# Softmax denominators by two VectorE instructions a unit in place of a ones-matmul, and the last token tile's transposes earlier, in a one-core hybrid decoder block

## The chip, the cores and the metric

The kernel runs on one core of one Trainium2 chip. The metric is the device time of one execution in microseconds, taken as the median of the runs. Before the change it is 766.99 us over three runs (766.61 to 769.15).

## What is computed

A sequence of 1024 tokens, with 16 meta tokens in front (1040 in all), width 1024, goes through one block of two parallel mixers. Everything is float32. Cut to what matters here:

```
h = rmsnorm(x, norm_g);  proj = h @ w_in            # u_pool z_pool q k v z_attn f g_pool g_attn
y_pool = multiscale_pool(u_pool) * silu(z_pool)     # trailing means over 2, 4, 8, 16 tokens
log_f  = log_sigmoid(f + b_forget);  c = cumsum(log_f)
s = q.k / 8 + c[query] - c[key], causal;  p = softmax(s)   # 8 heads of 64
y_attn = (p @ v) * silu(z_attn)
merged = sigmoid(g_pool) * (y_pool @ w_up_pool) + sigmoid(g_attn) * (y_attn @ w_up_attn)
out = rmsnorm(x + merged @ w_out, final_norm_g)      # meta positions dropped
```

The change is about two pieces of it: the sum over the keys in the softmax, and the order of the work on the last tile of `h`.

## The kernel before

Every large product is made of three float32r matmuls: each operand is split into a high part and a low part, and high*high, high*low and low*high are accumulated in PSUM (`g_mm3`, L134 to L140; the matmul itself is L139). One call of `g_proj` is one piece: 24 matmuls over 8 slices of the width.

**The start (L352 to L445)** is written out by hand, for all engines: each engine runs its instructions in the order of the code. Nine token tiles `xt` (the last has 16 tokens) are loaded, scaled (`norm_scale`, VectorE, L176) and transposed on TensorE (`norm_t`, L187) into PSUM tiles: of the two halves of each tile, every third goes to `pn`, of which there is one buffer, the others to `pt`, of which there are two. ScalarE evicts the high part (`hh`, L189), VectorE the low part (`hl`, L190), and with that the buffer is free. Between the tiles stand twelve pieces: q, k and v of the first head pair over four quarters of the tokens, numbered n = 0 to 11 in the loop at L411. The tiles come in by the table of L420: the last tile, number 8, is transposed after n = 8 (v of tokens 512 to 768), and first needed by n = 9 (q of tokens 768 to 1040). After the loop the small weights `wf` of the forget gate are split on VectorE (`wfs`, L443 and L444), and `gates` (L447) multiplies by them (L456).

**Attention** has 16 units: head pair p, head e, half of the queries. Keys lie on partitions, queries on the free axis, in blocks of 128 keys: 5 blocks in a first half ("even" units), 9 in a second ("odd" units). For each block `qk` makes scores into `ps` (L540, L541, two buffers) and evicts them to `S` (ScalarE L549, VectorE L547 on the masked part), with a running maximum `m` on VectorE. `maxes` turns `m` into a maximum for each query (transpose L561, reduce L563, small steps, transpose L571 into a `pt` buffer). `soft` subtracts it (VectorE L580), takes exp (ScalarE L581), splits into `ph` (ScalarE L584) and `pl` (VectorE L585) and adds up `acc` on GpSimd (L590, L591, L593); `av` (L601) multiplies by V two blocks later. The blocks of `soft` of a unit are interleaved with those of `qk` of the next unit.

`finish` closes a unit: it evicts the output (L608, L609), folds the 128 rows of `acc` to 64 (ScalarE L614, VectorE L615), splits the fold into a high and a low half (ScalarE L616, VectorE L617), and leaves a function `total` that one or two steps into the next unit sums over the partitions with a matmul of ones (L621), copies the row out (ScalarE L623) and stores it to DRAM in `sums`.

TensorE's order is written by hand throughout (`manual_schedule`); between the attention steps `F.pull` hands it pieces of other projections (q, k, v of the next pair, then the pooled inputs and the gates, spilled to DRAM by L295 and L305), as many nanoseconds of them as a table of costs says, and `F.drain` (L687) runs what is left. The other engines are ordered by the framework's scheduler, which sees the data and the `after` hints (an order on one engine, no wait).

**The tail** reloads what was spilled, makes the pooling mixer, reads `sums` back as `lall`, takes reciprocals (L830), stores them in `recs`, multiplies them into the attention output (`attn_out`), and runs the two up projections (`up`, a = 0 for pool, 1 for attention) and the output projection (L892).

Of the kernel before, what the change touches and what calls it, by code (L numbers as in the profile page):

```python
# [19 lines left out]
H = 8  # L20
# [19 lines left out]
NRC = 2  # L40
REC0 = 2
EVAC = (((0, 1),), ((0,), (1,)))
# [3 lines left out]
def r32(ap):  # L46
    return ap.bitcast(F32)
# [7 lines left out]
def tile_hybrid_block(ctx, tc, x, meta, norm_g, w_in, b_forget, pool_w, pool_scale,  # L55
# [355 lines left out]
    for n, (kind, t0, t1) in enumerate(todo):  # L411
        if n + 4 < 9:
            xts[n + 4] = norm_load(n + 4)
        if kind == "q":
            run(q_piece(0, wq, max(NM, t0), t1))
        elif kind == "k":
            run(k_piece(0, wk, t0, t1))
        else:
            run(v_piece(0, wv, t0, t1))
        i = {0: 2, 1: 3, 3: 4, 4: 5, 6: 6, 7: 7, 8: 8}.get(n)  # L420
        if i is not None:
            norm_t(i, xts[i], ntok(i))
# [16 lines left out]
    nc.sync.dma_start(psc, pool_scale[0].rearrange("(g c) -> c g", c=128))  # L439
    wf = sm.tile([128, KO, H], F32, name="wf", bufs=1)  # L440
    nc.sync.dma_start(wf, w_in2[:, :, COL_F:COL_F + H])
    wfs = sm.tile([128, KO, 2 * H], F32R, name="wfs", bufs=1)
    nc.vector.tensor_copy(wfs[:, :, :H], wf)  # L443
    nc.vector.tensor_tensor(wfs[:, :, H:], wf, r32(wfs[:, :, :H]), op=ALU.subtract)  # L444
    SM.close()  # L445

    def gates():  # L447
# [13 lines left out]
        for b in range(NB):  # L461
            nc.tensor.transpose(pt[:, b * 16:(b + 1) * 16], fT[:, KS[b]:KS[b] + KB], ident[:16, :16])
        z, lf, u, d, one, car = [sm.tile([KB, NB, H], F32, name=n, bufs=1) for n in ("fz", "lf", "fu", "fd", "fo", "car")]
        pv = pt[:, :NB * 16].rearrange("p (b j h) -> p b j h", j=2, h=H)
# [33 lines left out]

    exps, dves = [], []
    sums = dr.tile([H, SEQ], F32, name="sums")  # L500
    recs = dr.tile([H, SEQ], F32, name="recs")
    for p in range(4):
        spill["y", p] = dr.tile([128, SEQ], F32, name=f"sp_y{p}")

    class Unit:
# [19 lines left out]
        def qk(self, b):  # L525
# [22 lines left out]
            if f0 < 512:  # L548
                nc.scalar.activation(s[:kb, f0:], ps[:kb, f0:], AF.Identity, bias=nb_)  # L549
            S0 = self.S[0]  # L550
# [23 lines left out]
        def soft(self, b):  # L574
            kb, c0 = self.kb[b], self.c0[b]
            s = self.S[b]
            if b == 0:
                self.po = psO.tile([128, 512], F32, name="po")
                self.acc = ap_.tile([KB, 512], F32, name="acc", bufs=2)
            nc.vector.tensor_tensor(s[:kb, c0:], s[:kb, c0:], self.pm[:kb, c0:], op=ALU.subtract)  # L580
            exps.append(nc.scalar.activation(s[:kb, c0:], s[:kb, c0:], AF.Exp))  # L581
# [3 lines left out]
            dves.append(nc.vector.tensor_tensor(pl[:kb, c0:], s[:kb, c0:], r32(ph[:kb, c0:]), op=ALU.subtract))  # L585
            self.P[b] = (ph, pl)
            acc, S0 = self.acc, self.S[0]
            if b == 1:
                if c0:
                    nc.gpsimd.tensor_copy(acc[:, :c0], S0[:, :c0])  # L590
                nc.gpsimd.tensor_tensor(acc[:, c0:], S0[:, c0:], s[:, c0:], op=ALU.add)  # L591
            elif b > 1:
                nc.gpsimd.tensor_tensor(acc[:kb, c0:], acc[:kb, c0:], s[:kb, c0:], op=ALU.add)  # L593
            if b >= LAG:
                self.av(b - LAG)
# [8 lines left out]
        def finish(self):  # L604
# [5 lines left out]
            nc.sync.dma_start(spill["y", self.p][hr, self.q0:self.q0 + 512], t[hr])  # L610
            fold = ap_.tile([128, 512], F32R, name="ph", bufs=NPH)
            up_ = r32(ap_.tile([128, 512], F32R, name="pl", bufs=NPH))
            nu = KB - 64
            nc.scalar.copy(up_[:nu], acc[64:])  # L614
            nc.vector.tensor_tensor(acc[:nu], acc[:nu], up_[:nu], op=ALU.add)  # L615
            nc.scalar.activation(fold[:64], acc[:64], AF.Copy)  # L616
            nc.vector.tensor_tensor(fold[64:], acc[:64], r32(fold)[:64], op=ALU.subtract)  # L617

            def total():
                pr = psT.tile([128, 512], F32, name="pt")  # L620
                nc.tensor.matmul(pr, onesr, fold, start=True, stop=True)  # L621
                ls = ap_.tile([1, 512], F32, name="ls")
                nc.scalar.copy(ls, pr[:1])  # L623
                h = 2 * self.p + self.e
                nc.sync.dma_start(sums[h:h + 1, self.q0:self.q0 + 512], ls)

            return [total]

    def merged(a, c, extra=()):
        extra = list(extra)  # L630
        out_ = []
        for lst in (a, c):
            tot = sum(s[0] for s in lst) or 1
            acc = 0.0
            for s in lst:
                out_.append(((acc + 0.5 * s[0]) / tot, s))
                acc += s[0]
        for i, (_, (w, dve, pe, f)) in enumerate(sorted(out_, key=lambda t: t[0])):
            f()
            if i >= REC0 and extra:  # L640
                extra.pop(0)()
            F.pull(max(0.0, PACE * dve - pe))
# [22 lines left out]
    units[0].maxes(FIRST)  # L665
    late = []
    for i, u in enumerate(units):
        nxt = units[i + 1] if i + 1 < 16 else None
        F.now = i
        if nxt is not None and nxt.p != u.p:  # L670
            F.until(f"q{nxt.p}", f"k{nxt.p}")
        merged(list(nxt.a_steps()) if nxt else [], list(u.c_steps()), late)
        for b in range(u.nb - LAG, u.nb):
# [5 lines left out]
        if nxt is not None:  # L679
            nxt.maxes()  # L680
        late = u.finish()
        if nxt is not None and nxt.p != u.p:
            F.until(f"v{nxt.p}")
            pair_fill(nxt.p + 1)
    for f in late:
        f()
    F.drain()  # L687
# [47 lines left out]
    def attn_out(p):  # L735
        rc = btile("rc")
        for e in range(2):
            h = 2 * p + e
            after(nc.sync.dma_start(rc[rows(e)[0]], recs[h:h + 1, :].to_broadcast([64, SEQ])), stores[-1])
        nc.vector.tensor_tensor(Y[p], Y[p], rc, op=ALU.mult)  # L740
# [217 lines left out]
```

## Time and profile before

| | |
|---|---|
| profiled execution, its own time | 769.11 us |
| its span, first to last instruction | 767.4 us |
| runs: median, lowest, highest | 766.99, 766.61, 769.15 us |
| TensorE matmul busy | 751.6 us, 98% |
| TensorE weight loads busy | 638.5 us, 83% |
| VectorE busy | 497.1 us, 65% |
| ScalarE busy | 394.6 us, 51% |
| GpSimd busy | 278.1 us, 36% |
| mean granted TensorE clock | 0.997 |

Engines in the rows are PE (matmuls), PEld (weight loads), DVE (VectorE), ACT (ScalarE), POOL (GpSimd) and SP (the DMA queue of the sync engine); L139 is a line of the kernel. A row of a timeline has the start and the length in microseconds, the engine, the line, the operation, the tiles written and read, and in brackets the idle time before it and what ended that. A row of a group has, after the bar, the busy time of the group, the mean nanoseconds of one instruction, and the idle time before them. The clock column of a table of stretches is the share of full speed that TensorE was granted.

### The profile page before, as it was taken

Reading aid. Unit: us, or ns where it says so; the run is one execution under the profiler, and the core shown is the slowest. Engines: PE = TensorE matmul, PEld = TensorE weight load, DVE = VectorE, ACT = ScalarE, POOL = GpSimd, SP = SyncE. Lnnn points to the kernel's source line nnn. Section 1 sums busy time; section 2 is a strip of 40 time slices with the busy share of each in tenths; the row PEclk is TensorE's granted clock in tenths of the full one; section 3 lists DMA queues with packets and bytes.
Section 4 is the critical chain, followed back from the end, with each engine's and each line's share of the span. In section 5 each row is a group of like instructions: output and inputs, shape, how many; then the busy total and the mean of one; then the engine's idle time right before and its main releaser. Section 6 shows DMA issues by size and latency. Waiting matters only on the chain.

```text
span 767.4 us, 10526 instructions
## 1 busy us (share of the span) xinstructions
PE 751.6 (98%) x3762; PEld 638.5 (83%) x3762; DVE 497.1 (65%) x933; ACT 394.6 (51%) x756; POOL 278.1 (36%) x227
## 2 busy tenths in 40 slices
PE   8999999999999999999999999999999999999996
PEld 6996989988888898888988888888888688888885
DVE  5653578659779888598688866882465566434232
ACT  6652556456566655665655556551744554323112
POOL 4321235346326435433354263342374122322111
PEclk9999999999999999999999999999999999999999
DMA  9301122231221222221223232339357654523331
GB/s 304 73 18 39 28 82 74 67 97 49 62 58 52 72 75 70 77 63 41 77 62 103 71 103 62 103 108 373 123 176 177 233 176 128 191 83 113 107 110 55
DMA packets 73782, 79.33 MB, mean 103 GB/s; under 512 B 5473, under 2 KB 56673, under 8 KB 73730
## 3 DMA queue, kind: packets, MB, share of 16 engines
q1 hardware_dynamic: 68976, 63.46, 27.0%
q10 hardware_dynamic: 4754, 15.21, 6.0%
q8 instruction: 29, 0.48, 0.3%
q14 instruction: 23, 0.19, 0.1%
HBM read 57.58 MB, written 21.07 MB: 102 GB/s over the span
## 4 chain that ended last, share of the span: by engine, by line
PE 79%; DVE 8%; ACT 2%; issue 2%; DMA 2%; POOL 1%; POOLq 0%; DVEq 0%; SPq 0%; ACTq 0%
PE pj L139 57%; PE pj L892 12%; PE po L601 4%; PE ps L541 2%; PE ps L540 2%; DVE pl L585 1%; DVE S L580 1%; DMA rl<-sp_gp 1%; PE pj L456 1%; DVE ka L243 1%; POOL yl L722 1%; ACT S L549 1%; DMA rc<-recs 1%; DVE m L556 1%; DVE acc L615 0%
## 5 line engine op out<-in xcount | busy, mean ns | idle before, releaser
L139 PE MATMUL pj<-hh,whi 128*128 128x512 f32 (+4 forms) x768 | 179.9, 362 | 1.7 <-ACT hh L189 1.1
L139 PE MATMUL pj<-hl,whi 128*128 128x512 f32 (+4 forms) x768 | 178.0, 361 | 0.0
L139 PE MATMUL pj<-hh,wlo 128*128 128x512 f32 (+4 forms) x768 | 175.7, 360 | 0.0
L128 POOL TENSOR_TENSOR wlo<-raw,whi 128x1024 fp32r<-128x1024 f32 x37 | 91.7, 2478 | 223.7 <-ACT whi L127 90.5
L139 PEld LDWEIGHTS pj<-hh,whi 128*128 128x128 f32 x768 | 132.8, 190 | 19.6 <-ACT hh L189 1.2
L139 PEld LDWEIGHTS pj<-hh,wlo 128*128 128x128 f32 x768 | 133.2, 190 | 18.2
L139 PEld LDWEIGHTS pj<-hl,whi 128*128 128x128 f32 x768 | 132.5, 190 | 17.7
L585 DVE TENSOR_TENSOR pl<-S,ph 128x512 fp32r<-128x512 f32 (+4 forms) x112 | 87.1, 793 | 19.9 <-ACT ph L584 18.9
L593 POOL TENSOR_TENSOR acc<-acc,S 128x272 f32<-128x272 f32 (+4 forms) x80 | 77.5, 969 | 12.6 <-ACT S L581 6.6
L549 ACT ACTIVATE S<-ps,negc 128x400 f32<-128x400 f32 (+2 forms) x96 | 49.1, 515 | 46.7 <-DVE S L547 40.4
L581 ACT ACTIVATE S<-S 128x512 f32<-128x512 f32 (+4 forms) x112 | 49.4, 477 | 29.0 <-DVE S L580 28.9
L556 DVE TENSOR_TENSOR m<-m,S 128x272 f32<-128x272 f32 (+4 forms) x80 | 46.7, 583 | 22.3 <-ACT S L549 21.0
L584 ACT ACTIVATE ph<-S 128x512 fp32r<-128x512 f32 (+4 forms) x112 | 52.4, 478 | 11.6 <-PE po L601 10.8
L580 DVE TENSOR_TENSOR S<-S,pt 128x512 f32<-128x512 f32 (+4 forms) x112 | 51.7, 498 | 0.8
L892 PE MATMUL pj<-woh,gl 128*128 128x512 f32 (+1 forms) x136 | 51.8, 381 | 0.0
L892 PE MATMUL pj<-wol,gh 128*128 128x512 f32 (+1 forms) x136 | 51.6, 379 | 0.0
L892 PE MATMUL pj<-woh,gh 128*128 128x512 f32 (+1 forms) x136 | 51.6, 379 | 0.0
L816 POOL TENSOR_TENSOR gl<-rl,gh 128x512 fp32r<-128x512 f32 x16 | 23.2, 1454 | 72.3 <-ACT gh L815 72.3
L294 ACT ACTIVATE st<-pj 128x512 f32<-128x512 f32 x48 | 28.4, 592 | 39.7 <-PE pj L139 21.5
L127 ACT ACTIVATE whi<-raw 128x1024 fp32r<-128x1024 f32 x37 | 39.0, 1054 | 17.2 <-PE pj L139 10.6
L812 DVE TENSOR_TENSOR rl<-pj,rl 128x512 f32<-128x512 f32 x32 | 22.0, 689 | 31.8 <-PE pj L139 28.4
L540 PE MATMUL ps<-qa,ka 128*128 128x512 f32 (+4 forms) x112 | 36.4, 325 | 2.2 <-ACT S L549 2.1
(168 smaller groups left out, 1136.4 us busy)
## 6 DMA issues: line engine op xcount, KB each, us to landing
raw<-in_w_in_dram SPq DMA_DIRECT2D x40, 512.0 KB, 4.0
sp_gp<-st SPq DMA_DIRECT2D x16, 256.0 KB, 2.0
sp_ga<-st SPq DMA_DIRECT2D x16, 256.0 KB, 4.5
rl<-sp_gp ACTq DMA_DIRECT2D x8, 512.0 KB, 3.8
rl<-sp_ga ACTq DMA_DIRECT2D x8, 512.0 KB, 4.6
rawo<-in_w_out_dram SPq DMA_DIRECT2D x8, 512.0 KB, 3.1
xr<-in_x_dram SPq DMA_DIRECT2D x8, 512.0 KB, 4.3
xt<-in_x_dram SPq DMA_DIRECT2D x7, 512.0 KB, 8.3
```

The source lines that it names most:

```text
L127: nc.scalar.activation(hi, raw, AF.Copy)
L128: (eng or nc.gpsimd).tensor_tensor(lo, raw, r32(hi), op=ALU.subtract)
L139: nc.tensor.matmul(ps, a, b, start=(i == 0), stop=(i == len(seq) - 1))
L540: nc.tensor.matmul(ps[:kb, c0:], ka[:, k0:k0 + kb], qa[:, q0 + c0:q0 + 512], start=True, stop=False)
L549: nc.scalar.activation(s[:kb, f0:], ps[:kb, f0:], AF.Identity, bias=nb_)
L556: nc.vector.tensor_tensor(m[:kb, c0:], m[:kb, c0:], s[:kb, c0:], op=ALU.max)
L580: nc.vector.tensor_tensor(s[:kb, c0:], s[:kb, c0:], self.pm[:kb, c0:], op=ALU.subtract)
L581: exps.append(nc.scalar.activation(s[:kb, c0:], s[:kb, c0:], AF.Exp))
L584: nc.scalar.activation(ph[:kb, c0:], s[:kb, c0:], AF.Copy)
L585: dves.append(nc.vector.tensor_tensor(pl[:kb, c0:], s[:kb, c0:], r32(ph[:kb, c0:]), op=ALU.subtract))
L593: nc.gpsimd.tensor_tensor(acc[:kb, c0:], acc[:kb, c0:], s[:kb, c0:], op=ALU.add)
L892: nc.tensor.matmul(ps[:, :c1 - c0], mg[k][a][:, r], wo[k][b][:, c0:c1], start=(k == 0 and n == 0), stop=(k == KO - 1 and n == 2))
```

## The change

In words: `finish` no longer folds `acc` and no longer leaves a `total`. It transposes `acc` on VectorE in 32x32 blocks into an `mt` tile, reduces it to 128x16, and stores that in `sums`; an `after` puts the transpose behind the unit's last `pl` in VectorE's order. The tail reads `sums` back in four DMAs, one a head pair, sums over the four partition groups, takes the reciprocal, transposes back and stores `recs`. The first exp of a unit is put, in ScalarE's order, behind the last score eviction that was recorded before it. The last token tile is transposed after n = 7 in place of n = 8. `wf` is loaded after n = 4 and split after n = 8. The five small gate tiles become one, so that the tail can reuse its buffer.

The short description of the change also names "four pool up projections ahead of attention's". The diff does not touch `up` or its loop, and TensorE's order there is the same in both kernels: pool's projections 0, 1 and 2, then attention's 0, then alternating.

```
-        i = {0: 2, 1: 3, 3: 4, 4: 5, 6: 6, 7: 7, 8: 8}.get(n)
+        i = {0: 2, 1: 3, 3: 4, 4: 5, 6: 6, 7: 7}.get(n)
         if i is not None:
             norm_t(i, xts[i], ntok(i))
+        if n == 7:
+            norm_t(8, xts[8], ntok(8))
...
+        if n == 4:
+            wf = sm.tile([128, KO, H], F32, name="wf", bufs=1)
+            nc.sync.dma_start(wf, w_in2[:, :, COL_F:COL_F + H])
+        if n == 8:
+            wfs = sm.tile([128, KO, 2 * H], F32R, name="wfs", bufs=1)
+            nc.vector.tensor_copy(wfs[:, :, :H], wf)
+            nc.vector.tensor_tensor(wfs[:, :, H:], wf, r32(wfs[:, :, :H]), op=ALU.subtract)
...
-                nc.scalar.activation(s[:kb, f0:], ps[:kb, f0:], AF.Identity, bias=nb_)
+                sevs.append(nc.scalar.activation(s[:kb, f0:], ps[:kb, f0:], AF.Identity, bias=nb_))
...
             exps.append(nc.scalar.activation(s[:kb, c0:], s[:kb, c0:], AF.Exp))
+            if b == 0:
+                after(exps[-1], sevs[-1])
...
-            fold = ap_.tile([128, 512], F32R, name="ph", bufs=NPH)
-            up_ = r32(ap_.tile([128, 512], F32R, name="pl", bufs=NPH))
-            nu = KB - 64
-            nc.scalar.copy(up_[:nu], acc[64:])
-            nc.vector.tensor_tensor(acc[:nu], acc[:nu], up_[:nu], op=ALU.add)
-            nc.scalar.activation(fold[:64], acc[:64], AF.Copy)
-            nc.vector.tensor_tensor(fold[64:], acc[:64], r32(fold)[:64], op=ALU.subtract)
-
-            def total():
-                pr = psT.tile([128, 512], F32, name="pt")
-                nc.tensor.matmul(pr, onesr, fold, start=True, stop=True)
-                ls = ap_.tile([1, 512], F32, name="ls")
-                nc.scalar.copy(ls, pr[:1])
-                h = 2 * self.p + self.e
-                nc.sync.dma_start(sums[h:h + 1, self.q0:self.q0 + 512], ls)
-
-            return [total]
+            at = ap_.tile([KB, 512], F32, name="mt")
+            after(nc.vector.transpose(at, acc), dves[-1])
+            r = sm.tile([128, 16], F32, name="sr")
+            nc.vector.tensor_reduce(r, at.rearrange("p (j b) -> p j b", b=32), axis=AX.X, op=ALU.add)
+            nc.sync.dma_start(sums[4 * self.p + 2 * self.e + self.half], r)
...
-    lall = sm.tile([128, 64], F32, name="lall", bufs=1)
-    nc.sync.dma_start(lall, sums.rearrange("h (a b) -> (h a) b", b=64))
-    after(nc.vector.reciprocal(lall, lall), split2)
-    nc.sync.dma_start(recs.rearrange("h (a b) -> (h a) b", b=64), lall)
+    for p in range(4):
+        nc.sync.dma_start(lall[32 * p:32 * p + 32],
+                          sums[4 * p:4 * p + 4].rearrange("u (a r) j -> r u a j", r=32))
+    after(nc.vector.tensor_reduce(rall.rearrange("p (u j) -> p u j", u=4), lall.rearrange("p u a j -> p u j a"),
+                                  axis=AX.X, op=ALU.add), split2)
+    nc.vector.reciprocal(rall, rall)
+    nc.vector.transpose(fin[:, 320:], rall)
+    nc.sync.dma_start(recs.rearrange("(b p) r -> p b r", p=128), rect)
```

Three places show what this does to the engines' order. First TensorE in the start, before the change, from the transposes of tile 7 (`pn`, then `pt`, 128 columns) to the first matmuls of piece n = 9 (272 columns); the 256-column rows between are piece n = 8, and L256 are two transposes of V:

```order
L187 MATMUL pn<-ident,xt 128x128 x4
L187 MATMUL pt<-ident,xt 128x128 x4
L256 MATMUL pj<-ident,vt 128x128 x2
L139 MATMUL pj<-hh_112,whi 128x256 x4
L139 MATMUL pj<-hh_113,whi 128x256 x4
L139 MATMUL pj<-hl_114,whi 128x256 x4
L139 MATMUL pj<-hl_115,whi 128x256 x4
L139 MATMUL pj<-hh_112,wlo 128x256 x4
L139 MATMUL pj<-hh_113,wlo 128x256 x4
L187 MATMUL pt<-ident,xt 128x16 x4
L187 MATMUL pn<-ident,xt 128x16 x4
L139 MATMUL pj<-hh_112,whi 128x272 x4
```

And the same stretch of TensorE in the changed kernel, where the lines of the code have other numbers:

```order
L186 MATMUL pn<-ident,xt 128x128 x4
L186 MATMUL pt<-ident,xt 128x128 x4
L186 MATMUL pt<-ident,xt 128x16 x4
L186 MATMUL pn<-ident,xt 128x16 x4
L255 MATMUL pj<-ident,vt 128x128 x2
L138 MATMUL pj<-hh_112,whi 128x256 x4
L138 MATMUL pj<-hh_113,whi 128x256 x4
L138 MATMUL pj<-hl_114,whi 128x256 x4
L138 MATMUL pj<-hl_115,whi 128x256 x4
L138 MATMUL pj<-hh_112,wlo 128x256 x4
L138 MATMUL pj<-hh_113,wlo 128x256 x4
L138 MATMUL pj<-hh_112,whi 128x272 x4
```

The eight 16-column transposes of the last tile moved ahead of piece n = 8, directly behind those of tile 7, so that all of piece n = 8 stands behind them. On VectorE the low-part evictions of the last tile (`hl`, 128x4x16) moved with them, ahead of two V evictions; everything before them is as it was.

Second, VectorE at the end of the second unit (0, 0, second half), before, from the last maximum of the next unit to the transposed maximum `pt`:

```order
L556 TENSOR_TENSOR m<-m,S 128x16
L561 STREAM_TRANSPOSE mt<-m 128x512
L615 TENSOR_TENSOR acc<-acc,pl 64x512
L563 TENSOR_REDUCE mr<-mt 128x16
L565 COPY mx<-mr 64x16 x2
L617 TENSOR_TENSOR ph<-acc,ph 64x512
L566 TENSOR_TENSOR ms<-mr,mx 128x16
L568 COPY my<-ms 32x16 x4
L569 TENSOR_TENSOR mz<-ms,my 128x16
L571 STREAM_TRANSPOSE pt<-mz 128x512
```

And in the changed kernel:

```order
L561 TENSOR_TENSOR m<-m,S 128x16
L566 STREAM_TRANSPOSE mt<-m 128x512
L568 TENSOR_REDUCE mr<-mt 128x16
L570 COPY mx<-mr 64x16 x2
L619 STREAM_TRANSPOSE mt<-acc 128x512
L571 TENSOR_TENSOR ms<-mr,mx 128x16
L621 TENSOR_REDUCE sr<-mt 128x16
L573 COPY my<-ms 32x16 x4
L574 TENSOR_TENSOR mz<-ms,my 128x16
L576 STREAM_TRANSPOSE pt<-mz 128x512
```

Two instructions for the sums stand among those of the maximum in both; they are others, and a little later.

Third, ScalarE at the start of the third unit (0, 1, first half), before; `S<-S` is an exp, `S<-ps` the eviction of scores of the next unit (the first two stand behind these rows), `st` and `whi` belong to the filling projections:

```order
L614 COPY pl<-acc 64x512
L616 ACTIVATE ph<-acc 64x512
L304 ACTIVATE st<-pj 128x384
L608 ACTIVATE t<-po 64x512
L581 ACTIVATE S<-S 128x512
L581 ACTIVATE S<-S 128x400
L584 ACTIVATE ph<-S 128x512
L304 ACTIVATE st<-pj 128x272
L584 ACTIVATE ph<-S 128x400
L581 ACTIVATE S<-S 128x272
```

And in the changed kernel:

```order
L303 ACTIVATE st<-pj 128x384
L615 ACTIVATE t<-po 64x512
L126 ACTIVATE whi<-raw 128x1024
L586 ACTIVATE S<-S 128x400
L303 ACTIVATE st<-pj 128x272
L586 ACTIVATE S<-S 128x272
L586 ACTIVATE S<-S 128x144
L586 ACTIVATE S<-S 128x16
L554 ACTIVATE S<-ps,negc 128x512
L586 ACTIVATE S<-S 128x512
L591 ACTIVATE ph<-S 128x512
L591 ACTIVATE ph<-S 128x400
```

The two copies of the fold are gone, and the unit's first exp stands behind the first score eviction of the next unit, with the exps of the other four blocks ahead of it. It is so in the eight even units; in the odd units the eviction that the exp stands behind is one of its own scores, long done.

More of the change, by code (lines that the diff above doesn't have):

```diff
@@ L40 @@
 NRC = 2
-REC0 = 2
 EVAC = (((0, 1),), ((0,), (1,)))
@@ L439, in tile_hybrid_block @@
     nc.sync.dma_start(psc, pool_scale[0].rearrange("(g c) -> c g", c=128))
[L440 to L444, printed above, removed]
     SM.close()
@@ L462, in gates @@
             nc.tensor.transpose(pt[:, b * 16:(b + 1) * 16], fT[:, KS[b]:KS[b] + KB], ident[:16, :16])
-        z, lf, u, d, one, car = [sm.tile([KB, NB, H], F32, name=n, bufs=1) for n in ("fz", "lf", "fu", "fd", "fo", "car")]
+        fz = sm.tile([KB, 384], F32, name="fz", bufs=1)
+        z, lf, u, d, one = [fz[:, n * NB * H:(n + 1) * NB * H].rearrange("p (b h) -> p b h", h=H) for n in range(5)]
+        car = sm.tile([KB, NB, H], F32, name="car", bufs=1)
         pv = pt[:, :NB * 16].rearrange("p (b j h) -> p b j h", j=2, h=H)
@@ L497, in tile_hybrid_block @@
     pwl = sm.tile([128, 4, 128], F32R, name="pwl", bufs=1)
-    exps, dves = [], []
-    sums = dr.tile([H, SEQ], F32, name="sums")
-    recs = dr.tile([H, SEQ], F32, name="recs")
+    exps, dves, sevs = [], [], []
+    sums = dr.tile([16, 128, 16], F32, name="sums")
+    recs = dr.tile([256, 32], F32, name="recs")
     for p in range(4):
@@ L610, in finish, with merged @@
             nc.sync.dma_start(spill["y", self.p][hr, self.q0:self.q0 + 512], t[hr])
-            fold = ap_.tile([128, 512], F32R, name="ph", bufs=NPH)
-            up_ = r32(ap_.tile([128, 512], F32R, name="pl", bufs=NPH))
-            nu = KB - 64
[L614 to L617, printed above, removed]
-            def total():
-                pr = psT.tile([128, 512], F32, name="pt")
-                nc.tensor.matmul(pr, onesr, fold, start=True, stop=True)
-                ls = ap_.tile([1, 512], F32, name="ls")
-                nc.scalar.copy(ls, pr[:1])
-                h = 2 * self.p + self.e
-                nc.sync.dma_start(sums[h:h + 1, self.q0:self.q0 + 512], ls)
-            return [total]
-    def merged(a, c, extra=()):
-        extra = list(extra)
+            at = ap_.tile([KB, 512], F32, name="mt")
[3 more added lines that the diff above has]
+            nc.sync.dma_start(sums[4 * self.p + 2 * self.e + self.half], r)
+    def merged(a, c):
         out_ = []
@@ L637, in merged @@
                 acc += s[0]
-        for i, (_, (w, dve, pe, f)) in enumerate(sorted(out_, key=lambda t: t[0])):
+        for _, (w, dve, pe, f) in sorted(out_, key=lambda t: t[0]):
             f()
-            if i >= REC0 and extra:
-                extra.pop(0)()
             F.pull(max(0.0, PACE * dve - pe))
@@ L665, in tile_hybrid_block @@
     units[0].maxes(FIRST)
-    late = []
     for i, u in enumerate(units):
@@ L671, in tile_hybrid_block @@
             F.until(f"q{nxt.p}", f"k{nxt.p}")
-        merged(list(nxt.a_steps()) if nxt else [], list(u.c_steps()), late)
+        merged(list(nxt.a_steps()) if nxt else [], list(u.c_steps()))
         for b in range(u.nb - LAG, u.nb):
@@ L680, in tile_hybrid_block @@
             nxt.maxes()
-        late = u.finish()
+        u.finish()
         if nxt is not None and nxt.p != u.p:
@@ L684, in tile_hybrid_block @@
             pair_fill(nxt.p + 1)
-    for f in late:
-        f()
     F.drain()
@@ L737, in attn_out @@
         for e in range(2):
-            h = 2 * p + e
-            after(nc.sync.dma_start(rc[rows(e)[0]], recs[h:h + 1, :].to_broadcast([64, SEQ])), stores[-1])
+            rw = recs.rearrange("(h c) r -> h (c r)", h=H)[4 * e + p:4 * e + p + 1]
+            after(nc.sync.dma_start(rc[rows(e)[0]], rw.to_broadcast([64, SEQ])), stores[-1])
         nc.vector.tensor_tensor(Y[p], Y[p], rc, op=ALU.mult)
@@ L827, in tile_hybrid_block @@
     silu(zp[2])
-    lall = sm.tile([128, 64], F32, name="lall", bufs=1)
-    nc.sync.dma_start(lall, sums.rearrange("h (a b) -> (h a) b", b=64))
-    after(nc.vector.reciprocal(lall, lall), split2)
-    nc.sync.dma_start(recs.rearrange("h (a b) -> (h a) b", b=64), lall)
+    fin = sm.tile([128, 384], F32, name="fin", tag="fz", bufs=1)
+    lall = fin[:, :256].rearrange("p (u a j) -> p u a j", u=4, a=4)
+    rall = fin[:, 256:320]
+    rect = fin[:, 320:].rearrange("p (b r) -> p b r", b=2)
+    for p in range(4):
[6 more added lines that the diff above has]
+    nc.sync.dma_start(recs.rearrange("(b p) r -> p b r", p=128), rect)
     pool_chain(1)
```

## The prediction

> **What bounds the kernel now.** I read the page first: the busy times, the chain that ended last, then the groups by line.
>
> ```profile
> PE 751.6 (98%) x3762; PEld 638.5 (83%) x3762; DVE 497.1 (65%) x933; ACT 394.6 (51%) x756; POOL 278.1 (36%) x227
> PE 79%; DVE 8%; ACT 2%; issue 2%; DMA 2%; POOL 1%; POOLq 0%; DVEq 0%; SPq 0%; ACTq 0%
> ...
> L621 PE MATMUL pt<-ph,onesr 128*128 128x512 f32 x16 | 6.4, 401 | 0.0
> ```
>
> TensorE is busy for 98% of the span and makes 79% of the chain. A busy TensorE need not be at its peak, so I looked at its waits, and at a stretch of the chain with nothing but matmuls of 512 columns.
>
> ```profile
> PE ps L540 <- ACT S L549: 2.1, 3, 1.1
> ...
> PE pj L456 <- DVE wfs L444: 0.9, 1, 0.9
> ...
> 601.13 70.96 PE pj L139 x304
> ```
>
> Named waits of TensorE are a few single microseconds. 304 matmuls in 70.96 us are 233 ns each: what one more or one fewer 512-column matmul costs where TensorE never waits. In attention it hardly does. The first block of the third unit shows why:
>
> ```profile
> 151.04 1.17 DVE L580 TENSOR_TENSOR S<-S,pt 128x512 f32<-128x512 f32 x2
> ...
> 151.77 1.06 ACT L581 ACTIVATE S<-S 128x512 f32<-128x512 f32 x2 [1.37 <-DVE S L580]
> ...
> 153.38 1.61 DVE L585 TENSOR_TENSOR pl<-S,ph 128x512 fp32r<-128x512 f32 x2
> 154.01 0.40 PE L540 MATMUL ps<-qa,ka 128*128 128x512 f32 x1
> ...
> 155.68 0.68 ACT L549 ACTIVATE S<-ps,negc 128x512 f32<-128x512 f32 x1
> ...
> 158.65 0.69 DVE L554 TENSOR_TENSOR m<-S 128x512 f32<-128x512 f32 x1 [3.58 <-ACT S L549]
> ...
> 164.21 0.39 PE L601 MATMUL po<-ph,V 128*128 128x512 f32 x1
> ```
>
> The exps run from 151.77, the first `pl` is made by about 154.2 (half of the two from 153.38), and TensorE needs it behind the row at 164.21, 10 us later. So what is taken from TensorE is time saved; what is taken from ScalarE or VectorE in attention saves almost nothing, and costs nothing until such slack is used up.
>
> **The ones-matmuls.** Sixteen go. At 233 ns each that is 3.7 us, all of it on the path, since their group had no idle time before it (0.0). The last one cost more:
>
> ```profile
> 513.10 0.26 PE L601 MATMUL po<-pl,V 128*128 128x16 f32 x1
> 513.38 0.50 PE L621 MATMUL pt<-ph,onesr 128*128 128x512 f32 x1
> 513.72 1.32 PE L139 MATMUL pj<-hh,whi 128*128 128x512 f32 x5
> ```
>
> It started 0.28 us behind the matmul before it, which has 16 columns, and gave way after 0.34: 0.3 to 0.4 us beyond its 233 ns. Sum: **-4.1 us** (ends -3.5 and -4.5).
>
> **The fold and its successors.** Per unit:
>
> ```profile
> L615 DVE TENSOR_TENSOR acc<-acc,pl 64x512 f32<-64x512 f32 x16 | 12.4, 778 | 0.5 <-ACT pl L614 0.2
> L617 DVE TENSOR_TENSOR ph<-acc,ph 64x512 fp32r<-64x512 f32 x16 | 11.8, 738 | 0.3
> L561 DVE STREAM_TRANSPOSE mt<-m 128x512 f32<-128x512 f32 x16 | 11.3, 706 | 0.3
> L563 DVE TENSOR_REDUCE mr<-mt 128x16 f32<-128x512 f32 x16 | 10.8, 675 | 0.2
> L616 ACT ACTIVATE ph<-acc 64x512 fp32r<-64x512 f32 x16 | 10.1, 633 | 16.2 <-DVE acc L615 14.5 <-DVE ms L566 1.7
> L614 ACT COPY pl<-acc 64x512 f32<-64x512 f32 x16 | 9.9, 618 | 2.7 <-PE po L601 2.4
> L623 ACT COPY ls<-pt 1x512 f32<-1x512 f32 x16 | 9.0, 563 | 5.1 <-POOL pwl L678 5.0
> ```
>
> VectorE loses 778 + 738 and gains 706 + 675 ns, the prices of the same two operations on `m`: 0.14 us less, 16 times 2.2 us. ScalarE loses 633 + 618 + 563 ns, 29 us in all. Neither engine is late for TensorE, so I count 0 (ends -1.5, if the ScalarE wait of 2.1 us above shrinks, and +0.5). The new transpose sits in VectorE's queue in front of the next unit's `pt` and all its exps, and waits for GpSimd's `acc`. In the tightest unit, the sixth:
>
> ```profile
> 245.87 3.85 POOL L593 TENSOR_TENSOR acc<-acc,S 128x400 f32<-128x400 f32 x4
> ...
> 252.08 0.71 DVE L561 STREAM_TRANSPOSE mt<-m 128x512 f32<-128x512 f32 x1
> ```
>
> `acc` ends at 249.72 and the transpose comes after `mt` at 252.08, so this wait is 2.4 us from biting. The `sums` stores become 128 short pieces, and four reloads wait on SP for such stores to land, with weight loads and spills queued behind them. In no row of its waits does TensorE wait for a weight split of these pieces (`whi`, `wlo`) or for a spilled bank, so a few microseconds on SP stay hidden: 0. The tail's extra reduce and transpose fall into VectorE's wait for `u` behind the reciprocals:
>
> ```profile
> 548.91 1.24 DVE L757 TENSOR_TENSOR s<-u 128x1039 f32<-128x1039 f32 x1 [3.83 <-DMA u<-sp_u]
> ```
>
> **The first exp.** In the third unit it moves from 151.77 to behind the eviction of scores that TensorE finishes at about 154.7: some 4 us later, against 10 us of slack. The eviction itself comes earlier than its 155.68. The merged gate tiles change no wait. Count 0.
>
> **The last tile, sooner.** Here the change gives back. These are rows of the start, with the clock of the same stretch:
>
> ```profile
> 42.62 1.19 PE L139 MATMUL pj<-hh,whi 128*128 128x256 f32 x8
> ...
> 43.23 1.39 DVE L176 SCALAR_TENSOR_TENSOR xt<-xt,rstd,gb 16x512 f32<-16x512 f32 x2 [0.65 <-POOL rstd L111]
> ...
> 45.52 0.69 DVE L190 TENSOR_TENSOR hl<-pn,hh 128x512 fp32r<-128x512 f32 x1
> ...
> 46.27 0.42 PE L187 MATMUL pn<-ident,xt 16*128 16x16 f32 x4 [0.24 <-DVE hl L190]
> ...
> 47.77 1.27 PE L139 MATMUL pj<-hh,whi 128*128 128x272 f32 x8 [1.08 <-ACT hh L189]
> ...
> 52.26 1.31 PE L139 MATMUL pj<-hh,whi 128*128 128x272 f32 x8
> ...
> 55.54 1.25 PE L139 MATMUL pj<-hh,whi 128*128 128x272 f32 x8
> ...
> 59.66 1.54 PE L456 MATMUL pj<-hh,wfs 128*16 128x384 f32 x8 [0.86 <-DVE wfs L444]
> ```
>
> ```profile
> 49.00:50.00 1.00, 1.00 (x8) 1.00 (x7) 0.00 (x0) 0.00 (x0) 0.00 (x0) 0.58 0.00 0
> 50.00:51.00 1.00, 1.00 (x6) 1.00 (x6) 0.00 (x0) 0.27 (x1) 0.00 (x0) 0.50 0.00 0
> 51.00:52.00 1.00, 1.00 (x6) 1.00 (x6) 0.00 (x0) 0.79 (x1) 0.00 (x0) 0.50 0.08 16
> 52.00:53.00 1.00, 1.00 (x8) 1.00 (x7) 0.00 (x0) 0.49 (x2) 0.40 (x1) 0.71 0.00 0
> ```
>
> Before, piece n = 8 ran from 42.62 to about 45.6, and only then came the last tile's transposes. The second four of them need the one `pn` buffer, which VectorE frees with the row that ends at 46.21; they start at 46.27. Nothing ahead of that row on VectorE or ScalarE moved. In the new order TensorE stands ready at about 42.4, waits for the scaled tile until about 43.9 (the first half of the 43.23 row), and then for the same 46.27, with all of piece n = 8 behind. The piece then starts at about 46.8 and ends, after the same 3.0 us, at 49.8, where n = 9 can start at once: 2.0 us later than 47.77. The wait of 0.86 us for `wfs` goes, because its split now comes three pieces earlier than its use. Without the clock: **+1.1 us**.
>
> The clock: in these rows about 3.4 us stand at half speed, behind a stretch in which TensorE had 1.08 us idle and transposes. It cost 4.49 us for n = 9 (47.77 to 52.26) against 3.28 for n = 10: 1.2 to 1.3 us. The longer hold of the new order makes a half-speed stretch as well; on the same 3.4-us grid it covers 46.0 to 49.4, of which TensorE works 2.6 us, at the same rate about 1.0 us. If the grid lies elsewhere, one stretch meets 2 to 3.4 us of its work and two in a row nearly 5: 0.7 to 1.8. The Trainium skill (page "TensorE: Matmul & The Clock Gate", table in "Why this matters for your kernels") tells to avoid idle gaps over about 3 us; by that neither order would be slowed, the credit of 1.3 and the debit of 1.0 would both go, the start would stay at +1.1 and the sum at -3.0. The trace disagrees: 1.08 us of idle and two sets of transposes were enough. Its "Part 1" says that the window is free-running, which no run here shows yet.
>
> Start in all: +1.1 + 1.0 - 1.3 = **+0.8 us** if the run before has its half-speed stretch, as the profiled one has, **+2.1** if it has not.
>
> **The sum.** -4.1 + 0.8 = -3.3 us on the profiled execution: 769.11 becomes 765.8. That execution lies 2.1 us above the median of 766.99 and next to the slowest run, so the median may well be a run without the stretch, for which the sum is -4.1 + 2.1 = -2.0. I take the middle, -2.6 on the median: **764.4 us**. About 0.3%, 2.3 us, is what a measurement of this kernel can tell from no change; the forecast is just past it.
>
> **Rivals.**
> - *The start costs more* (0.17): two half-speed stretches in a row, or a slip of VectorE's queue, 1.5 us more than I count: 765.9, no change. For it: the hold of 4.4 us is longer than a 3.4-us stretch. Against: one stretch was seen.
> - *The last tile's hold does not arise* (0.09): `pn` is free sooner, the transposes hide, and the 1.1 us idle and the 0.9 for `wfs` are gained: -4.1 - 2.0 = -6.1, and -7.4 where the half-speed stretch goes too; the middle, -6.8, is 760.2. Against: the 46.27 row starts right on the row that ends at 46.21.
> - *The ones-matmuls were free* (0.05): TensorE would have waited there in any case, and only the start counts, +0.8 to +2.1: 768.4, no change. Against: 0.0 idle around them.
> - *Slower* (0.06): ScalarE in the even units now stands still behind a score eviction that TensorE has not produced, and VectorE's `pl` behind it, ahead of the next unit's maxima. The hold is about 3 us, eight times. In the third unit `pl` would be made at about 157.2 (154.7, then 0.6 each for eviction, exp, `ph` and `pl`), against maxima from 158.65. From the point where it comes after them it goes into the next, odd unit; 0.8 us in each would be +6.4, with -2.6: 770.8.
> - *The change does what its words don't say*: they name pool's up projections; TensorE's order there is the same in both, so neither sum nor chance has a part of it.
>
> **How the numbers follow.** Forecast 0.63, its own range 763.0 to 766.0 (the ends of the ones-matmuls and of the clock); about 0.41 of the chance lies past the 2.3 us. Faster: 0.41 + 0.09 = 0.50. Same: 0.22 + 0.17 + 0.05 = 0.44. Slower: 0.06. The range for 8 in 10 holds the forecast and the costlier start with their ends and leaves out the other three, 0.20: 761.8 to 767.0.
>
> **What would show it.** Right: no row of a ones-matmul, and the drain behind the last unit starts 3 to 4 us sooner relative to the first matmul by `wfs`; TensorE idle between 42.4 and 46.8, its last four transposes at 46.3 released by the `hl` row; a half-speed stretch just behind; the first matmul by `wfs` at 60 to 61 with no wait. Wrong: piece n = 8 starting before 44, or new TensorE waits over 1 us in the odd units, released by `pl`.

## The result and the profile after

The changed kernel takes 772.29 us (median of 5 runs, 771.01 to 774.10), the kernel before 767.33 us (766.61 to 769.15, 5 runs). The ratio is 1.0062, 95% interval 1.0042 to 1.0082: slower by 0.6%, about 4.8 us. The forecast was 764.4 us.

The profiled executions differ less, 769.11 us before and 771.90 us after, because the one before has a half-speed stretch that, by their granted clocks, most runs of that kernel don't have (the last section). So times below are compared by the ratio of the runs with its interval, and profiles only for where a wait stands.

From the page after, the busy times and the chain (the work that ended last, followed back from the end) by engine:

```profile
PE 750.6 (97%) x3746; PEld 637.2 (83%) x3746; DVE 509.6 (66%) x935; ACT 368.9 (48%) x708; POOL 279.5 (36%) x227
PE 71%; DVE 13%; ACT 4%; issue 3%; DMA 1%; POOL 1%; POOLq 0%; ACTq 0%; DVEq 0%; SPq 0%
```

The sixteen ones-matmuls are gone (3746 matmuls, before 3762), and ScalarE works 26 us less. Yet TensorE's share of the chain fell from 79% to 71%, and VectorE's and ScalarE's rose from 10% to 17%: the end is now held more often by what TensorE waits for. Its waits after:

```profile
PE ps L545 <- ACT S L554: 4.4, 6, 1.3
PE po L608 <- DVE pl L592: 2.2, 2, 1.6
PE pn L186 <- DVE hl L189: 1.8, 1, 1.8
PE pt L186 <- issue: 1.4, 1, 1.4
```

Before, the wait for ScalarE's evictions of the scores (`S`) was 2.1 us in three places, that for `pl` 0.3 in one, that of `pn` for `hl` 0.2, and the last did not exist. Four numbers, three causes. First the start; these are TensorE's rows:

```profile
43.69 0.39 PE L186 MATMUL pt<-ident,xt 16*128 16x16 f32 x4 [1.42 <-issue]
45.90 0.60 PE L186 MATMUL pn<-ident,xt 16*128 16x16 f32 x4 [1.82 <-DVE hl L189]
...
46.77 2.06 PE L138 MATMUL pj<-hh,whi 128*128 128x256 f32 x8
...
51.80 1.16 PE L138 MATMUL pj<-hh,whi 128*128 128x272 f32 x8
...
61.02 1.56 PE L459 MATMUL pj<-hh,wfs 128*16 128x384 f32 x8
```

As forecast, the last tile's transposes wait for the scaled tile (the profile names no releaser; VectorE scales that tile from 42.85 to 44.24) and then for the `hl` row, and piece n = 8 starts at 46.77. Eight matmuls of 256 columns take 2.06 us, where they took 1.19. The clock in stretches (the 0.50 behind the engines' busy times is its share of full speed):

```profile
44.70:48.10 3.40, 2.20 (x12) 2.17 (x13) 2.36 (x7) 0.78 (x3) 0.00 (x0) 0.50 0.00 0
48.10:51.50 3.40, 3.40 (x18) 3.40 (x18) 0.61 (x3) 0.00 (x0) 0.00 (x0) 0.50 0.00 0
...
109.50:112.90 3.40, 3.40 (x13) 3.20 (x13) 2.99 (x5) 2.25 (x4) 1.56 (x3) 0.50 0.16 58
```

Two half-speed stretches in a row in the start, and a third at 109.5 us, in attention, which the profile before doesn't have. What stands ahead of it are the first blocks of the softmax. Before:

```profile
103.85 0.61 ACT L584 ACTIVATE ph<-S 128x512 fp32r<-128x512 f32 x1
104.37 0.67 ACT L549 ACTIVATE S<-ps,negc 128x512 f32<-128x512 f32 x1
...
106.70 1.25 ACT L549 ACTIVATE S<-ps,negc 128x512 f32<-128x512 f32 x2
107.42 0.50 PE L540 MATMUL ps<-qa,ka 128*128 128x512 f32 x1 [0.73 <-ACT S L549]
```

And after, with the score matmul that waits for it:

```profile
105.70 0.67 ACT L554 ACTIVATE S<-ps,negc 128x512 f32<-128x512 f32 x1
106.27 0.72 ACT L586 ACTIVATE S<-S 128x512 f32<-128x512 f32 x2
...
106.92 1.38 ACT L591 ACTIVATE ph<-S 128x512 fp32r<-128x512 f32 x3
...
108.57 1.25 ACT L554 ACTIVATE S<-ps,negc 128x512 f32<-128x512 f32 x2
109.30 0.64 PE L545 MATMUL ps<-qa,ka 128*128 128x512 f32 x1 [1.28 <-ACT S L554]
```

There are two `ps` buffers. A score matmul needs the eviction of the one two before it, and that eviction now stands on ScalarE behind two exps, three `ph` and a spill copy `st`. From the first eviction's start to the second's there were 2.33 us (104.37 to 106.70) and are 2.87 (105.70 to 108.57), and the wait grew from 0.73 to 1.28 us. The rest of what the waits for `S` gained stands in the other even units: 0.4 us at 225.7, 0.3 more at 269.7, 0.8 at 375.9 and 0.3 at 428.2.

### The profile page after: what moved, and what is told of

It reads as the page before. It is cut to its first block, busy times and chain, and to the rows that moved or that the text cites. A ratio compares the mean times of both kernels' runs of the same rounds, so it can differ in the third digit from the quotient of the medians.

```text
span 770.1 us, 10480 instructions
## 1 busy us (share of the span) xinstructions
PE 750.6 (97%) x3746; PEld 637.2 (83%) x3746; DVE 509.6 (66%) x935; ACT 368.9 (48%) x708; POOL 279.5 (36%) x227
## 4 chain that ended last, share of the span: by engine, by line
PE 71%; DVE 13%; ACT 4%; issue 3%; DMA 1%; POOL 1%; POOLq 0%; ACTq 0%; DVEq 0%; SPq 0%
PE pj L138 51%; PE pj L889 12%; PE po L608 4%; DVE pl L592 2%; DVE S L585 2%; PE ps L546 2%; PE ps L545 2%; ACT S L554 1%; DVE m L561 1%; PE pj L459 1%; DVE ka L242 1%; DMA rl<-sp_gp 1%; DVE S L552 1%; DVE pt L576 1%; DVE mx L570 1%
## 5 line engine op out<-in xcount | busy, mean ns | idle before, releaser
L592 DVE TENSOR_TENSOR pl<-S,ph 128x512 fp32r<-128x512 f32 (+4 forms) x112 | 92.5, 848 | 36.4 <-ACT ph L591 35.9
L600 POOL TENSOR_TENSOR acc<-acc,S 128x272 f32<-128x272 f32 (+4 forms) x80 | 79.4, 993 | 10.8 <-ACT S L586 5.4
L586 ACT ACTIVATE S<-S 128x512 f32<-128x512 f32 (+3 forms) x112 | 49.8, 479 | 48.4 <-DVE S L585 48.0
L561 DVE TENSOR_TENSOR m<-m,S 128x272 f32<-128x272 f32 (+4 forms) x80 | 49.0, 612 | 20.7 <-ACT S L554 18.0
```

The costliest lines, as they stand in the source:

```text
L561: nc.vector.tensor_tensor(m[:kb, c0:], m[:kb, c0:], s[:kb, c0:], op=ALU.max)
```

## The experiments

Twelve kernels were run, each with a profile, 4 to 12 times beside the kernel before. Ratios are to the kernel before, with their 95% intervals; the changed kernel stands at 1.0062. Microseconds behind a ratio are its distance from 1 times 767. By these intervals the difference of two kernels is uncertain by about 1 us among e1, e2, e3 and e9, and by up to about 2 us where the changed kernel, e5, e8, e10, e11 or e12 is one of them.

**e1, the whole change without the hint.**

```
             exps.append(nc.scalar.activation(s[:kb, c0:], s[:kb, c0:], AF.Exp))
-            if b == 0:
-                after(exps[-1], sevs[-1])
```

> The changed kernel without the hint that puts a unit's first exp behind the next unit's first score eviction. Theory A (the hint makes ScalarE late with the score evictions, because the first exp, its split and its neighbours then stand in one lump ahead of the second eviction): TensorE's waits for S at 107, 109, 225, 268, 375 and 427 us go, and with them the half-speed stretch at 110 to 113: 0.8 + 0.5 + 0.9 + 0.4 for the waits and 2.0 for 109 us, 4.6 us, so 767.7 us, and the granted clock about 0.995. Theory B (the sums on VectorE, ahead of the next unit's transposed maximum, make softmax late): the waits stay, 772 us. Theory C (all of the loss is the start): 772 us as well.

Measured: 769.07 us, 1.0018 (1.0009 to 1.0026), 3.4 us below the changed kernel. The waits:

```profile
PE ps L545 <- ACT S L554: 2.1, 3, 1.1
...
PE pj L138 <- ACT whu L782: 1.1, 1, 1.1
```

The waits for `S` are back at 2.1 us, so the hint was the cause of what they had gained; theories B and C fall as the whole story. It gave 3.4 and not 4.6 us: the profiled run still has a stretch of half speed from 108.1 us, and in the tail 1.1 us of waiting for `whu` stands where the changed kernel, coming later, had none.

**e2, the whole change with the last tile back behind n = 8.**

```
-        i = {0: 2, 1: 3, 3: 4, 4: 5, 6: 6, 7: 7}.get(n)
+        i = {0: 2, 1: 3, 3: 4, 4: 5, 6: 6, 7: 7, 8: 8}.get(n)
...
-        if n == 7:
-            norm_t(8, xts[8], ntok(8))
```

> The changed kernel with the last tile's transposes back behind n = 8. All theories give the start back; they differ in how much. By the two profiles the first matmul by the forget weights was 1.4 us later in the changed kernel, although the wait for wfs (0.9) was gone: theories A and B say 772.3 - 1.4 - 0.9 = 770.0 us, 770.7 if the half-speed stretch of the kernel before comes back with the wait of 1.1 us. Theory C: all 5 us come back, 767.3 us.

Measured: 769.40 us, 1.0023 (1.0012 to 1.0034): 3.0 us come back, between the 2.3 of A and the 5 of C. The start is a second cause, beside the hint.

**e3, both of these edits.**

```
-            if b == 0:
-                after(exps[-1], sevs[-1])
...
-        if n == 7:
-            norm_t(8, xts[8], ntok(8))
```

> The changed kernel without the hint and with the last tile back behind n = 8: what is left of the change are the sums on VectorE, the earlier forget weights and the merged gate tile. Theory A: 767.7 - 2.3 = 765.4 us, below the kernel before, because sixteen ones-matmuls (16 x 233 ns = 3.7) are gone against about 1.8 us of new waits for pl at 246 and 360 us. Theory B: about 770 us. Theory C: 767.3 us.

Measured: 765.82 us, 0.9977 (0.9966 to 0.9988), 1.8 us faster than before, as A said. The parts add up: from e3, the hint (e2) costs 3.5 us and the last tile (e1) 3.1; -1.8 + 3.5 + 3.1 = +4.8 us, the changed kernel. Of the hint's 3.5 us the profiles show 2.5 as waits for `S` (1.9 in e3, 4.4 in e2); the mean granted clock, 0.9961 over e3's runs and 0.9947 over e2's, fits another 1 us. But without the ones-matmuls and the wait for `wfs` 5 us should be gone. The waits say where the rest went:

```profile
PE po L604 <- DVE pl L588: 2.1, 2, 1.6
PE ps L543 <- ACT S L552: 1.9, 2, 1.1
```

The wait for `pl` was 0.3 us before. It has two places. In the sixth unit ScalarE's order before was (`ls` is the copy of the sums, `whi` a weight split for a later piece):

```profile
238.34 0.58 ACT L623 COPY ls<-pt 1x512 f32<-1x512 f32 x1
238.82 0.63 ACT L584 ACTIVATE ph<-S 128x512 fp32r<-128x512 f32 x1
...
241.99 1.04 ACT L127 ACTIVATE whi<-raw 128x1024 fp32r<-128x1024 f32 x1
```

And in e3:

```profile
234.41 1.04 ACT L126 ACTIVATE whi<-raw 128x1024 fp32r<-128x1024 f32 x1
235.36 0.62 ACT L587 ACTIVATE ph<-S 128x512 fp32r<-128x512 f32 x1
...
238.54 0.50 PE L604 MATMUL po<-pl,V 128*128 128x512 f32 x1 [0.52 <-DVE pl L588]
```

With `ls` gone the scheduler put the weight split ahead of the `ph`. The `ph` itself was still in time: it ended at 235.98, and VectorE came to its `pl` at 236.77, which beside the same TensorE matmuls is only 0.1 us later than before. But that `pl` took longer. Before, with GpSimd's low part `wlo` of the weight split:

```profile
241.24 0.69 DVE L585 TENSOR_TENSOR pl<-S,ph 128x512 fp32r<-128x512 f32 x1
243.11 2.80 POOL L128 TENSOR_TENSOR wlo<-raw,whi 128x1024 fp32r<-128x1024 f32 x1
```

And in e3:

```profile
235.53 2.41 POOL L127 TENSOR_TENSOR wlo<-raw,whi 128x1024 fp32r<-128x1024 f32 x1
236.77 1.72 DVE L588 TENSOR_TENSOR pl<-S,ph 128x512 fp32r<-128x512 f32 x1
```

The earlier split let GpSimd start `wlo` ahead of the `pl`, which then ended 0.55 us behind it (238.49 against 237.94). In the tenth unit the scheduler put VectorE's third `pl` ahead of a maximum and four subtractions. It too ran beside GpSimd (336.77, 1.78 us, where before it took 0.69), VectorE came about 1.3 us later to what follows, and the wait there is 1.59 us. That GpSimd's work is what made the two `pl` long is read from these rows; no run tries it alone.

**e4, the kernel before with only the hint added.**

```
...
             exps.append(nc.scalar.activation(s[:kb, c0:], s[:kb, c0:], AF.Exp))
+            if b == 0:
+                after(exps[-1], sevs[-1])
```

> The kernel before with nothing but the hint on the first exp added. Theory A: the new waits for S and the half-speed stretch at about 108 us come in, 767.3 + 4.6 = 771.9 us. Theory B and theory C: 767.3 us, no change.

Measured: 768.69 us, 1.0012 (1.0002 to 1.0023): slower by 0.9 us, not by 4.6.

```profile
PE ps L540 <- ACT S L549: 3.1, 3, 1.3
```

The hint alone adds 1.0 us of waiting for `S`, with the sums on VectorE 2.5 (1.9 in two places in e3, 4.4 in six in e2). So A has the mechanism, but its size depends on what else the scheduler has to place; why the fold's copies soften it was not tried by itself.

**e5, e3 with two order hints at the two places of `pl`.**

```
+            sub = nc.vector.tensor_tensor(s[:kb, c0:], s[:kb, c0:], self.pm[:kb, c0:], op=ALU.subtract)
+            if F.now == 9 and b == 8:
+                after(dves[-6], sub)
...
+            phs.append(nc.scalar.activation(ph[:kb, c0:], s[:kb, c0:], AF.Copy))
...
+        if F.now == 5:
+            after(act, phs[-2])
```

> The kernel of e3 (sums on VectorE, no hint, last tile behind n = 8) with two order hints and nothing else: in the sixth unit the weight split on ScalarE goes behind the last but one split of an exp that was recorded, in the tenth unit the third pl on VectorE goes behind the subtraction of its last block, as it stood in the kernel before. Theory D (the gain that is missing in e3 against the ones-matmuls' 4.1 us is lost at these two places, because the scheduler put other work ahead when ScalarE's copies had gone): the two waits for pl, 0.6 and 1.6 us, go, so 765.8 - 2.1 = 763.7 us. Theory E (the transpose and reduce of acc on VectorE are themselves the cost, wherever they stand): no change, 765.8 us.

Measured: 763.09 us, 0.9932 (0.9913 to 0.9951), 3.4 us below e3. The waits for `pl` are down to 0.2 us:

```profile
PE ps L547 <- ACT S L556: 2.1, 3, 1.1
...
PE po L610 <- DVE pl L594: 0.2, 1, 0.2
```

D holds: not the new instructions but the order that the scheduler made around them was the cost. -5.2 us (-3.8 to -6.7) is what the removed matmuls (4.1 by the forecast) and the removed wait for `wfs` (0.9) come to; these, the merged gate tile and the tail's new steps were not run apart. That it gained 3.4 where the waits for `pl` fell by 1.9 stays open: the mean granted clock was the same (0.9961 over e3's runs, 0.9960 over e5's), and the difference of 1.5 lies within the uncertainty of 1.7.

**e6 and e7, the last tile's eight transposes in one `pt` buffer.** In e6 on e1, where the change put them:

```
+            both = psT.tile([128, 8, 64], F32, name="pt")
...
+                pt = both[:, 4 * j:4 * j + 4]
```

In e7 on e3, and inside piece n = 8 (`pc`):

```
+            if n == 8:
+                for _ in range(18):
+                    next(pc)
+                norm_t(8, xts[8], ntok(8))
+            run(pc)
```

> The kernel of e1 (the whole change without the hint) with all eight transposes of the last tile in one pt buffer, so that none needs pn. Theory F (TensorE's hold in the start is the wait for pn, freed at about 46.2 us): the transposes run at 43.7 to 44.5, the 1.8 us wait on the hl row goes, the 1.4 us wait for the scaled tile stays; 769.1 - 1.9 = 767.2 us. Theory G (the clock alone makes the start dear, and a hold of 1.4 us brings the half-speed stretch as well): 768.5 us or more.

> The kernel of e3 with the last tile's eight transposes in one pt buffer and put behind the 18th of the 24 matmuls of piece n = 8, where the tile is scaled and the rest of the piece covers the evictions. Theory F: no hold at n = 8 and no wait of 1.1 us for hh at n = 9, and the half-speed stretch of the start becomes rare: 765.8 - 1.1 - 0.4 for the small waits on pt and hl = 764.3 us, up to 0.5 less for the clock. Theory G (the stretch comes from the transposes, which go on): 764.7 us.

Measured: e6 770.04 us, 1.0022 (1.0013 to 1.0032), the same as e1; e7 768.75 us, 1.0002 (0.9988 to 1.0016), 1.9 us worse than e3. In e6:

```profile
46.96 0.60 PE L190 MATMUL pt<-ident,xt 16*128 16x16 f32 x4 [2.55 <-DVE hl L193]
```

F falls: without `pn` the second four wait even longer, 2.55 us, now for the `hl` row of the first four. Both buffers are freed by an eviction that stands behind the scaling of the tile, two `ka` rows and two more `hl` rows on VectorE. e7 carries the same wait, 2.50 us, into the middle of a piece.

**e8, e7 with order hints for the two places, that of the sixth unit in another form.**

```
+            if F.now == 5 and b == 3:
+                after(splits[-1], ph_)
```

> The kernel of e3 with the last tile inside piece n = 8 as in e7, and the order hints in another form: in the sixth unit the weight split recorded last goes behind the split of the fourth block's exp, in the tenth unit as in e5. Theories D and F together: 765.8 - 1.5 for the start - 1.4 to - 2.1 for the two places = 762.5 us. If D is wrong, 764.3 us.

Measured: 773.77 us, 1.0059 (1.0036 to 1.0082), the slowest of the twelve by its median.

```profile
PE pj L140 <- ACT whi L128: 4.7, 1, 4.7
```

This form held another split, the one whose product TensorE needed next, and from 237.5 us, still in that wait, the clock stands at half for two stretches, to 244.3. It tells nothing about D or F.

**e9, e1 with the eight transposes ahead of both evictions.**

```
+            for i in range(8):
+                nc.tensor.transpose(pt[:, i, :n], xt[:n, i * 128:(i + 1) * 128], ident[:n, :n])
+            for j in range(2):
...
```

> The kernel of e1 (the whole change without the hint) with all eight transposes of the last tile into one pt buffer ahead of both its evictions. In e6 the second four waited 2.5 us for the hl row of the first four, which stood behind 4 us of VectorE's queue. Theory H (the hold of the start is VectorE's queue, through whatever eviction the second four wait for): now they wait for the scaled tile alone, piece n = 8 starts at about 45.2 in place of 47.0, and the time is 769.1 - 1.8 = 767.3 us. Theory G (a hold of 1.4 us with transposes costs a half-speed stretch just so): 768.5 us or more.

Measured: 767.00 us, 0.9986 (0.9977 to 0.9995), 2.5 us below e1.

```profile
44.55 0.42 PE L183 MATMUL pt<-ident,xt 16*128 16x16 f32 x4 [0.23 <-DVE xt L175]
44.90 0.50 PE L264 MATMUL pj<-ident,vt 128*128 128x128 f32 x2
```

H holds: with no eviction between the two sets the V transposes ahead of piece n = 8 run at 44.90, where e1's trace has 46.61, and the time is 2.5 us less.

**e10, e5 with these eight transposes inside piece n = 8.** The edits are those of e9 and of e7.

> The kernel of e5 (sums on VectorE, two order hints) with the eight transposes in one pt buffer, ahead of both evictions, behind the 18th matmul of piece n = 8. Theory H: no hold, no wait of 1.1 us for hh at n = 9, no 0.4 us of small waits: 763.1 - 1.5 = 761.6 us, and the half-speed stretch of the start mostly gone, up to 0.5 less. Theory G: 762.7 us or more, the stretch as often as in e5.

Measured: 762.61 us, 0.9933 (0.9918 to 0.9949): no different from e5. The transposes no longer wait, but the wait for `hh` stayed:

```profile
47.34 0.28 ACT L273 ACTIVATE V<-pj 128x128 fp32r<-128x128 f32 x1 [3.40 <-DVE V L274]
...
47.78 0.99 PE L142 MATMUL pj<-hh,whi 128*128 128x272 f32 x5 [1.02 <-ACT hh L190]
```

ScalarE's `hh` stands behind a V eviction that waits 3.40 us for VectorE. H's second half, that n = 9 would not wait, was wrong: VectorE's queue reaches TensorE by another way.

**e11, e5 with the hint on the split in place of the exp.**

```
+                if b < 2 and self.half == 0:
+                    after(phs[-1], sevs[-1 - b])
```

> The kernel of e5 with another hint in the place of the change's: in the even units not the exp but its split into the high part goes behind a score eviction, that of the first block behind the first eviction, that of the second block behind the second. ScalarE then runs four exps, an eviction, one split, an eviction, and the other splits. Theory A (what counts is how soon ScalarE evicts the scores, and the change's hint put one exp and three splits ahead of the second eviction): the waits for S fall from 2.1 us to 0.6 or less, 763.1 - 1.5 = 761.6 us, and the half-speed stretch at 106 us gets rarer. Rival I (any hint that holds ScalarE behind an eviction loses, because pl comes late): 764 to 767 us.

Measured: 760.78 us, 0.9909 (0.9893 to 0.9924), the fastest, 7 us below the kernel before.

```profile
99.90 1.59 ACT L590 ACTIVATE S<-S 128x512 f32<-128x512 f32 x4
...
101.40 0.67 ACT L556 ACTIVATE S<-ps,negc 128x512 f32<-128x512 f32 x1
...
102.97 1.25 ACT L556 ACTIVATE S<-ps,negc 128x512 f32<-128x512 f32 x2
```

The second eviction starts 1.57 us behind the first (101.40 to 102.97), against 2.87 after the change and 2.33 in e5. TensorE waits for `S` once, 1.2 us, in the place of three waits of 2.1; no half-speed stretch comes in this profile before its last 1.3 us. Rival I, which had at least 764 us, falls, and the waits are as A said: holding ScalarE's softmax behind an eviction is good or bad by what then stands ahead of the second eviction. The gain on e5 in time, 1.8 us, is not clear of the noise by itself (uncertain by 1.9).

**e12, e10 and e11 together.**

> The kernel of e5 with both e10's place of the last tile and e11's hints. If H and A both hold, the gains add: 763.1 - 3.0 = 760.1 us. If only one holds, 761.6 us.

Measured: 761.06 us, 0.9910 (0.9897 to 0.9923): as e11. The last tile inside the piece adds nothing, as in e10.

## Why the prediction was wrong

- **The ones-matmuls, -4.1 us: right, as far as e5 shows.** In e5 they and the wait for `wfs` are gone and little else is in the way; it is 5.2 us faster, against 4.1 + 0.9.
- **The last tile, sooner: right in mechanism and in its sum.** Forecast were +2.0 us of hold (apart from `wfs`) and +1.0 for the clock, 3.0; measured 3.1 (e1 against e3) and 3.0 (changed kernel against e2). How it divides between hold and clock is less sure: the profile after has the two half-speed stretches in a row that the prediction gave to a rival, e1's has one. (By the clock rows that the prediction shows, the stretch that it takes from 46.0 to 49.4 lies at 45.8 to 49.2, which changes its 1.0 us by 0.1.) The credit of 1.3 for the stretch of the kernel before was wrong for the median: by their clocks about a third of its runs have such a stretch, and the prediction's second case, +2.1 for the start, was the one to take. That the one `pn` buffer makes the hold was too narrow: e6 has the same hold with a `pt` buffer, through an eviction in VectorE's queue, and e9, with no eviction between the transposes, has not.
- **"The fold and its successors: 0": wrong by 3.4 us** (e3 against e5). The step took the removed ScalarE work as time that nobody waits for, which it was. It did not follow that the scheduler fills places that come free with something else: in the sixth unit a weight split ahead of a `ph`, in the tenth a `pl` ahead of four subtractions. The cost is no duration in the trace of before, where both `pl` took 0.69 us; it stands in the order of the changed kernel, which put them beside GpSimd's work, where they took 1.72 and 1.78, in two units with next to no slack before: the sixth, which the prediction called the tightest for another wait, and the tenth, in which TensorE already waited 0.3 us for `pl`. Of the 3.4 us the profiles show 1.9 as these waits.
- **"The first exp: count 0": wrong by 3.5 us** (e2 against e3). The step compared the exp with its consumer on TensorE, ten microseconds later. It did not ask what else is queued on ScalarE behind the lump that the hint makes: the second score eviction, for which TensorE has two buffers and, in the first unit, no slack: it already waited 0.73 us for it. The row for it, `PE ps L540 <- ACT S L549`, was the first among TensorE's waits, and the prediction quoted it.
- **The sum.** With the start at +2.1 it was -2.0 us; measured +4.8. The missing 6.8 are the two terms counted at nothing, 3.4 + 3.5.
- **The rival on the other side** named the engine and the units (ScalarE held in the even units, 770.8 us), but put the cost on `pl` in the next unit and gave it 0.06. The profile has it on `ps`, in the even units themselves. The sign set for it, a new wait of over 1 us for `pl` in an odd unit, did appear (1.59 us, in the tenth), but by another path: e3, without the hint, has it as well.
- **The sign for being right** failed in attention: the drain was to start 3 to 4 us sooner behind the first matmul by `wfs`. Between the two there were 454.1 us (59.66 to 513.72) and are 456.3 (61.02 to 517.35), 2.3 later. So the profiles put 5 to 6 us of what is missing between these two, in attention.

## What to carry to other kernels

Slack must be taken for every instruction that is queued behind a moved one on its engine, above all for the evictions of a two-buffer PSUM tile, and not only for the moved instruction's own consumer. Where a scheduler sets the order, removing cheap work is no smaller change than adding some: compare its order at the two or three tightest places, and if something else has slid into the gap, hold it with an order hint (here two hints were worth 3.4 us; a hint like the change's, on the split in place of the exp, gave perhaps 1.8 more). A hint that pins an instruction that TensorE needs next can cost more than the whole change.

## What the runs showed of the hardware

The half-speed stretches begin on a grid of 3.41 us, which lies elsewhere from run to run. In the profile after they begin at 44.7 and 109.5 us, 64.8 apart, 19 times 3.41. In e5:

```profile
44.80:48.20 3.40, 2.09 (x19) 1.76 (x18) 2.78 (x9) 0.79 (x4) 0.00 (x0) 0.99 0.00 0
48.20:51.60 3.40, 3.40 (x17) 3.40 (x16) 0.00 (x0) 0.73 (x1) 0.00 (x0) 0.50 0.00 0
...
102.80:106.20 3.40, 1.77 (x10) 1.46 (x11) 2.42 (x4) 3.40 (x10) 2.37 (x4) 1.00 0.00 0
106.20:109.60 3.40, 3.40 (x13) 3.21 (x14) 1.90 (x3) 2.29 (x4) 1.08 (x2) 0.50 0.16 58
```

48.2 and 106.2 are 17 times 3.41 apart, and in e1 46.7 and 108.1 are 18 times. Counted from the start of the span, a step of the grid falls at 0.3 us in the profile after, at 0.4 in e5, at 2.3 in e1 and, by its stretch from 49.2, at 1.4 in the profile before. The Trainium skill (page "TensorE: Matmul & The Clock Gate", "Part 1") says that the window is free-running and 3413 ns long; that agrees with these starts. In the step of the grid ahead of these half-speed stretches TensorE was busy for 1.4 us (from 41.2) and 1.8 (from 106.1) of 3.4 in the profile after, and for 2.1 and 1.8 in e5. No single wait in these steps took more than 1.5 us of them, so the idle gap of about 3 us that the same page's table in "Why this matters for your kernels" gives as the limit is too long for this kernel. Where the limit lies the runs don't show: in the profile before, the step from 103.8 has 1.8 us of work as well, and the clock stays at full speed behind it.

So where the grid lies looks like chance, and with it whether a short wait falls into one step of it or is shared by two. That fits the times. Of 35 runs of the kernel before beside e1 to e4, 24 had a mean granted clock of 0.998 or 0.999 and took 767.4 us in the mean; 11 had 0.996 or 0.997 and took 768.9. The 1.4 us between them fit the price of one stretch, for the same program; those runs left no profile that shows it.
